# HGRN2 score levels 2, 8 and 32 as 32-column matmuls on the array's four column groups

## The chip, the cores and the metric

The kernel runs on one core of a Trainium2 chip. The metric is the device time of one execution in microseconds. Three runs of the kernel before gave 2279.91, 2280.7 and 2283.08 us; the median is 2280.7 us. One further execution was profiled. It is the source of all rows of the trace below.

## The reference, cut to what matters

One layer of a hybrid decoder is run for 256 prompt tokens and 8 x 8 sample tokens, 320 columns in all. It has two token mixers, an mLSTM with 4 heads and an HGRN2 with 8 heads, fed by one input projection and followed by branch, output and feed-forward projections. The change lies in the scores `a` of the HGRN2 heads:

```python
G = jnp.cumsum(lfc, axis=2)
rel = G[:, :, :, None, :] - G[:, :, None, :, :]
rel = jnp.where(causal[:, :, None], rel, -jnp.inf)
a = jnp.sum(qc[:, :, :, None, :] * jnp.exp(rel) * kc[:, :, None, :, :], axis=-1)
o = jnp.einsum('bhts,bhsv->bhtv', a, ic) + jnp.einsum('bhtk,bhkv->bhtv', qc * jnp.exp(G), S)
```

For a pair of tokens s < t the weight is the product of the forget gates between them, channel by channel, times q of t and k of s, summed over 128 channels.

## The kernel before, in words

All weights are streamed once. A weight tile of 128 output columns comes in two units of 128 x 1024 numbers. ScalarE rounds a unit to a high part (`wh`, line 334), VectorE forms the low part (`wl`, line 504), and TensorE multiplies both parts by the 320 token columns, three products for each of the 16 steps over 2048 rows. So a unit is 24 matmuls with a moving operand of 320 columns. This stream, called the main stream here, runs from the first microseconds to nearly the end. Everything else is slipped in between.

The order of all engines is written out by a planner when the program is built. Each piece of side work is a generator (a chain) that yields requests: an engine with a cost in ns and the instructions, a wait for an event, or a buffer of a pool. `Sched.pump` is called after each step of the main stream. A side matmul is put into TensorE's order when the planner's clock has passed the time at which its inputs are due plus a lead of 450 ns. The planner's costs only set the order; on the chip, semaphores keep it.

The HGRN2 heads run while their input projections are streamed. The eight heads follow one another about every 49 us (line 1434 runs at 467.5, 517.5, 566.1 and so on to 759.8 us). For head h the chain `h_scan` forms cumulative gate products by doubling. On the way it writes, for the blocks B = 2, 8 and 32 of `QUADS`, a buffer `y` of 1024 columns from the pool `yb`, which holds one buffer. Columns 0 to 383 of it are k times its gate products, columns 384 on are q times its gate products, six blocks of B columns for every group of four blocks. The chain `h_a` turns each `y` into scores: for each 128 tokens one full matmul (lines 1542 to 1544) with the 128 columns of k as weights and 192 columns of q as moving operand (96 columns for the 64 sample tokens, which only B = 2 has). These are fp32 matmuls, which the profile shows as two passes each. A 128 x 192 product holds many entries that belong to no group of four blocks; three masked copies per level (line 1556) move the wanted ones from the bank to `at`. A level takes one bank of the pool `sbank` of six, makes its matmuls, gives `y` back, copies, gives the bank back, and the next level follows. A fifth buffer, for B = 128, comes from the same pool.

Around it stand `h_state`, which holds one bank and takes four more at once for the sample states, and the main stream's evictions, which have two banks of their own (`mbank`). When the last mLSTM head is done, `m_after` calls `carve_h`, which lays out the HGRN2 buffers over tiles that the mLSTM part used. There the tile `rxb`, which takes the memory `rx` of mLSTM states, is laid out for the branch inputs `bah` that `ev_o` writes after the heads.

Of the kernel before, what the change touches and what calls it, by code (L numbers as in the profile page):

```python
# [246 lines left out]
def post(ev):  # L247
    return ("set", ev)
# [19 lines left out]
PE_4 = 400.0  # L268
PE_C = 2000.0
PE_H = 1250.0  # L270


def cap(ap, off, dims):
# [22 lines left out]
class Program:  # L296
# [49 lines left out]
    def carve(self):  # L346
        class Part:
            def __init__(self, ap, lo=0):
                self.ap, self.o, self.end = ap, lo, ap.shape[1]

            def __call__(self, n, parts=128):
                self.o += n
                assert self.o <= self.end, (self.o, self.end)
                return self.ap[:parts, self.o - n:self.o]

            def three(self, a, b):
                return self(a * b).rearrange("p (a b) -> p a b", a=a)

        self.Part = Part
        A, B, C, R = Part(self.f1), Part(self.f2), Part(self.f3), Part(self.ra[:, 0:6400])  # L360

        self.hs = Pool([A(2048) for _ in range(3)])

        self.qk = Pool([A.three(4, 320) for _ in range(2)])
        self.vr = Pool([A(1280)])
        B2 = Part(self.f2a)
        self.kw = Pool([B2.three(2, 320)])
        self.bc = Pool([B2(712) for _ in range(2)])
        self.eb0 = B(512)
        self.eb = Pool([self.eb0])  # L370
        self.stg = Pool([B2(256), B(256)])
        self.qn0 = B(ODD + 256)
        self.qn = Pool([self.qn0])
        X = Part(self.rx)
        self.cb = Pool([C(512) for _ in range(6)] + [X(512) for _ in range(8)])
        self.hb0 = C.three(3, 512)
        self.hb = Pool([self.hb0])
        self.qz0 = C(ODD + 512)
        self.qz = Pool([self.qz0])
        self.tst = Pool([B(512)])  # L380
        self.tail = Pool([B(64) for _ in range(2)])
        self.tst2 = B(320)
        self.ss0 = self.ra[:, 6384:6384 + ODD + 256]
        self.shl = Pool([(R(384), R(384), self.ss0)])
        self.vhl = Pool([R(2048).rearrange("p (x n) -> p x n", x=2)])
        self.vs = Pool([R(512)])
        R(1024)
        self.kst = Pool([R.three(2, 256)])
        self.vst = Pool([R.three(2, 512)])

        A, B = Part(self.f1, 6144), Part(self.f2)
        self.sb = Pool([A.three(4, 256) for _ in range(2)])
        self.at = Pool([A(512) for _ in range(2)])
        self.yb0 = A(1024)
        self.yb = Pool([self.yb0])
        self.hstg0 = [B(128) for _ in range(2)]
        self.hstg = Pool(self.hstg0)
        self.on0 = B.three(3, 256)
        self.on = Pool([self.on0])
        self.ho = Pool([B(256) for _ in range(2)])  # L400
        self.tail2 = Pool([B(64) for _ in range(2)])
        R2 = Part(self.ra, 5120)
        self.hkst = Pool([R2.three(2, 128)])
        self.phl = Pool([(R2(512), R2(512))])
        self.hvs = Pool([self.ra[:, 6400:6656]])
        self.late = [B(320) for _ in range(4)]
        self.sg0 = B(320)
        self.sg = Pool([self.sg0, self.tst2])
        B = Part(self.f2, 2000)
        self.sr = Pool([B(320) for _ in range(2)])  # L410

        B = Part(self.f2)
        self.tmp = Pool([B(320) for _ in range(3)])
        self.xr = Pool([B(320) for _ in range(4)])

    def carve_h(self):
        C = self.Part(self.pool.tile([128, F3], F32, name="f3h", tag="f3"))
        qz = C(ODD + 256)
        self.hqz = Pool([qz])
        pp = C(512)  # L420
        self.pp = Pool([pp])
        self.ktk = Pool([C(256)])
        R = self.Part(self.pool.tile([128, 2320], F32R, name="f2r", tag="f2a"))
        self.it = Pool([[R(512) for _ in range(2)] for _ in range(2)])
        as_ = R(ODD + 256)
        self.ats = Pool([as_])
        for x in (qz, as_.bitcast(F32), *(x[:, 0:64] for x in self.hstg0), pp[:, 480:512], self.yb0[:, 320:384]):
            self.nc.gpsimd.memset(x, 0.0)
        self.rh = self.pool.tile([128, 512], F32R, name="rh", tag="rh")
        self.hvst = Pool([self.rh.rearrange("p (a b) -> p a b", a=2)])  # L430
        X, R = self.Part(self.pool.tile([128, 4096], F32R, name="rxb", tag="rx")), self.Part(self.ra)
        self.bah = Slices([(X if j < 12 else R)(TOK) for j in range(KT)])
        self.bal = Slices([R(TOK) for _ in range(KT)])
        now = self.s.t["pe"]
        self.hs.free.append((now, C(2048)))
        self.sb.free += [(now, C.three(4, 256)) for _ in range(2)]
        self.sg.free += [(now, self.sg0), (now, self.late[0])]
        self.sr.free.append((now, self.late[1]))
        self.ld = Pool(self.late[2:])

    def carve_m(self):

# [171 lines left out]
    def before(self, i, t):  # L614
        s = self.s
        kind, h, c = t[:3]
        if kind == "mv" and c == 0:
            s.until(lambda: self.vr.free and self.qk.free)
            self.m_start(h)
            self.vr.free.sort(key=lambda x: x[0])  # L620
            self.mh[h]["vr"] = self.vr.free.pop(0)[1]
        elif kind == "hf":
            s.until(lambda: self.hs.free)
            if h == 0:
                s.spawn(self.m_after(), 0)
            self.h_start(h)
        elif kind == "o" and h == 0:
            s.until(lambda: all(m["end"].t is not None for m in self.mh))
        elif kind == "hg" and h == 0:
            s.until(lambda: all(m["end"].t is not None for m in self.hh))  # L630
            self.carve_m()
            self.carve_b()
            f2 = self.pool.tile([128, 2320], F32, name="f2l", tag="f2a")
            B = self.Part(f2)
            for pool in (self.sg, self.sg, self.sr, self.ld, self.ld, self.ld):
                pool.free.append((s.t["pe"], B(320)))
            B = self.Part(f2)
            self.lnb = [B(320) for _ in range(7)]
# [22 lines left out]
    def start(self):  # L661
# [40 lines left out]
        self.bc_ev = [Ev() for _ in range(MH)]  # L702
        self.mh = [dict(end=Ev()) for _ in range(MH)]
        self.hh = [dict(end=Ev()) for _ in range(HH)]
        self.m_all = Ev()
        self.ba_ev = [Ev() for _ in range(KT)]
        self.bb_ev = [Ev() for _ in range(KT)]
        self.mg_ev = [Ev() for _ in range(KT)]
# [682 lines left out]
    def h_start(self, h):  # L1391
# [2 lines left out]
        a = m["set"] = self.hs.free.pop(0)[1]  # L1394
        a = self.Part(a)
        m["qk"], m["fs"], m["iv"] = a.three(2, 384), a.three(2, 320), a(640)
        for n in ("kst", "f", "q", "lv", "o", "pre8", "suf", "I", "V", "av", "SP", "S", "aT", "qz", "ist", "sdone", "got", "ld"):
            m[n] = Ev()
        m["i"] = [Ev(), Ev()]
        m["Y"] = [Ev() for _ in range(5)]  # L1400
# [60 lines left out]
    def h_scan(self, h):  # L1461
# [23 lines left out]
        for n, B in enumerate(QUADS):  # L1485
# [14 lines left out]
            yield from join(2 * B, T)  # L1500
            if B == 2:
                yield post(m["pre8"])
        y = m["y"][4] = yield acq(self.yb)
        for i in range(2):
            yield ("dve", dve(128), lambda: v.tensor_tensor(y[:, 128 * i:128 * i + 128], qk[:, i, 128 * i:128 * i + 128], fs[:, i, 128 * i:128 * i + 128], ALU.mult))
        yield post(m["Y"][4])
# [4 lines left out]
    def h_a(self, h):  # L1511
# [22 lines left out]
        yield ("dve", dve(192, True) + 150, lambda: v.copy_predicated(a3[:, :, 1:128:2], mk, b[:, TOK:TOK + 192].rearrange("p (a t) -> p a t", a=3)))  # L1534
        yield rel(self.sbank, b)
        at_mask = 64
        for n, B in enumerate(QUADS):
            yield wait(m["Y"][n + 1])
            y = m["y"][n + 1]
            b = yield acq(self.sbank)  # L1540
            w, g = (3 if B == 2 else 2), 128 // (4 * B)
            for i in range(w):
                k = 192 if i < 2 else 96
                yield ("pe", pe_f(k), lambda: self.mm(b[:, 192 * i:192 * i + k], y[:, 128 * i:128 * i + 128], y[:, 384 + 192 * i:384 + 192 * i + k], start=True, stop=True))
            yield rel(self.yb, y)
            for d in (1, 2, 3):
                k, o = (4 - d) * B, (0, 3, 5)[d - 1] * B
                if B == 2:
# [10 lines left out]
        y = m["y"][4]  # L1559
        b = yield acq(self.sbank)  # L1560
        yield ("pe", pe_f(128), lambda: self.mm(b[:, 0:128], y[:, 0:128], y[:, 128:256], start=True, stop=True))
        yield rel(self.yb, y)
        yield ("act", act(128, True), lambda: self.A(at[:, 384:512], b[:, 0:128]))
        yield rel(self.sbank, b)
        yield post(m["aT"])

    def h_i(self, h):
        m = self.hh[h]
# [252 lines left out]
    def ev_o(self, j, c, b):  # L1821
        v = self.nc.vector
        g = yield acq(self.sg)
        r = yield acq(self.sr)
        yield from self.sigmoid(b[:, :TOK], g, r, ((self.mbank, b),))
        yield rel(self.sr, r)
        x = yield from self.fetched("o", j)
        yield ("dve", dve(TOK), lambda: v.scalar_tensor_tensor(g, g, self.vec[:, V_MLG + j:V_MLG + j + 1], x, ALU.mult, ALU.mult))
        yield rel(self.ld, x)
        if j >= 12:  # L1830

            yield wait(*(m[e] for m in self.hh for e in ("av", "sdone")))
        yield from self.split(g, self.bah[:, j, :], self.bal[:, j, :])
        yield rel(self.sg, g)
        yield post(self.ba_ev[j])
# [400 lines left out]
```

## Time and profile before

| what | value |
|---|---|
| median of three runs | 2280.7 us |
| span of the profiled execution | 2278.2 us |
| TensorE matmul busy | 2268.4 us |
| VectorE busy | 1426.4 us |
| ScalarE busy | 1014.8 us |
| stage of the HGRN2 heads | about 445 to 817 us |

The profiled execution has no time of its own beside its span, which runs from its first to its last instruction; the runs' median is 2.5 us longer. In the rows below, PE is TensorE's matmuls, PEld its weight loads, DVE VectorE, ACT ScalarE. A matmul's row gives the partitions and columns of the weights in use (`128*32`) and the shape of the moving operand. Line 340 is the helper through which nearly all matmuls pass, so groups are told apart by their operands: `xh`, `xl` with `wh`, `wl` is the main stream; `bank<-f 128*128 128x192` and `128x96` are the score matmuls of the change, as `y` lies in the tile `f`.

In a timeline a row's duration contains the latency of a pipelined matmul. What a matmul costs the stream is read from the distance between starts.

### The profile page before, as it was taken

How to read it: one execution, taken by the hardware profiler on the slowest of the kernel's cores; microseconds unless marked ns; L12 is line 12 of the kernel's file. 1: busy time of each engine (PE TensorE's matmuls, PEld its weight loads, DVE VectorE, ACT ScalarE, POOL GpSimd, SP SyncE). 2: the span in 40 equal slices, each digit the busy share in tenths (PEclk: the TensorE clock that was granted, in tenths of full speed). 3: DMA queues.
4: the chain of work that ended last, by engine and by line, in shares of the span. 5: the costliest groups of instructions: out<-in, count | busy, mean ns of one | idle time of the engine just before them, and what ended most of it. 6: DMA issues, size and time to landing. Idle time of an engine off the chain costs nothing.

```text
span 2278.2 us, 39090 instructions
## 1 busy us (share of the span) xinstructions
PE 2268.4 (100%) x15546; PEld 2231.5 (98%) x15546; DVE 1426.4 (63%) x2490; ACT 1014.8 (45%) x1574; POOL 13.5 (1%) x42
## 2 busy tenths in 40 slices
PE   9999999999999999999999999999999999999998
PEld 9999999999999999999999999999999999999998
DVE  6767566798888877555555769444444444444566
ACT  5434444455555565444433447333433343234434
POOL 0000000000000000000000000000000000000000
PEclk9999999999999999999999999999999999999999
DMA  7887887677667764444555644444444444444644
GB/s 243 304 262 258 247 273 235 215 222 227 210 208 222 220 207 171 171 172 171 181 173 196 202 154 148 150 154 150 148 148 149 154 151 148 148 149 153 197 150 158
DMA packets 251167, 432.88 MB, mean 190 GB/s; under 512 B 106844, under 2 KB 146916, under 8 KB 250984
## 3 DMA queue, kind: packets, MB, share of 16 engines
q1 hardware_dynamic: 250088, 427.24, 56.5%
q0 software_dynamic: 896, 3.15, 0.5%
q8 instruction: 122, 2.00, 0.4%
q14 instruction: 61, 0.50, 0.1%
HBM read 377.30 MB, written 53.00 MB: 189 GB/s over the span
## 4 chain that ended last, share of the span: by engine, by line
PE 96%; DMA 1%; ACT 1%; DVE 1%; issue 0%; SPq 0%; ACTq 0%; POOL 0%; DVEq 0%; POOLq 0%
PE bank L340 96%; DMA wr<-wt 1%; ACT f3m L334 0%; ACT wh L334 0%; DVE wl L504 0%; SPq L343 0%; ACT oC L334 0%; PE bank L1117 0%; PE bank L1041 0%; DMA ksD<-ra 0%; PE bank L1315 0%; ACT f2l L334 0%; DVE f L1472 0%; ACT oS L334 0%; DVE f3m L2107 0%
## 5 line engine op out<-in xcount | busy, mean ns | idle before, releaser
L340 PE MATMUL bank<-xh,wh 128*128 128x320 f32 x2408 | 759.8, 317 | 0.0
L340 PE MATMUL bank<-xh,wl 128*128 128x320 f32 x2408 | 743.1, 310 | 0.0
L340 PE MATMUL bank<-xl,wh 128*128 128x320 f32 x2408 | 740.4, 309 | 0.0
L334 ACT ACTIVATE wh<-wr 128x1024 fp32r<-128x1024 f32 (+1 forms) x432 | 453.2, 1049 | 624.3 <-PE bank L340 571.4
L504 DVE TENSOR_TENSOR wl<-wr,wh 128x1024 fp32r<-128x1024 f32 x423 | 517.0, 1222 | 324.7 <-ACT wh L334 318.1
L340 PEld LDWEIGHTS bank<-xh,wh 128*128 128x128 f32 x2408 | 453.0, 188 | 6.1 <-issue 3.9
L340 PEld LDWEIGHTS bank<-xl,wh 128*128 128x128 f32 x2408 | 452.6, 188 | 2.6
L340 PEld LDWEIGHTS bank<-xh,wl 128*128 128x128 f32 x2408 | 452.9, 188 | 0.0
L334 ACT ACTIVATE bb<-wr 128x1024 fp32r<-128x1024 f32 x181 | 191.9, 1061 | 355.9 <-PE bank L340 340.1
L504 DVE TENSOR_TENSOR bb<-wr,bb 128x1024 fp32r<-128x1024 f32 x179 | 219.2, 1225 | 162.0 <-ACT bb L334 162.0
L340 PE MATMUL bank<-xh,bb 128*128 128x320 f32 (+1 forms) x1280 | 284.1, 309 | 0.0
L340 PE MATMUL bank<-ra,bb 128*128 128x320 f32 x1264 | 283.3, 308 | 0.0
L340 PE MATMUL bank<-rxb,bb 128*128 128x320 f32 x1112 | 255.0, 309 | 0.0
L340 PE MATMUL bank<-ra,wh 128*128 128x320 f32 x892 | 248.8, 308 | 0.0
L340 PEld LDWEIGHTS bank<-xh,bb 128*128 128x128 f32 x1280 | 214.6, 188 | 0.0
L340 PEld LDWEIGHTS bank<-ra,bb 128*128 128x128 f32 x1264 | 210.6, 188 | 0.2
L340 PE MATMUL bank<-xl,bb 128*128 128x320 f32 (+1 forms) x640 | 197.5, 309 | 0.0
L340 PEld LDWEIGHTS bank<-rxb,bb 128*128 128x128 f32 x1112 | 188.3, 188 | 0.2
L340 PE MATMUL bank<-rxb,wl 128*128 128x320 f32 x596 | 183.7, 308 | 0.0
L340 PE MATMUL bank<-rxb,wh 128*128 128x320 f32 x596 | 183.7, 308 | 0.0
L340 PEld LDWEIGHTS bank<-ra,wh 128*128 128x128 f32 x892 | 161.4, 188 | 0.0
L340 PEld LDWEIGHTS bank<-xl,bb 128*128 128x128 f32 x640 | 120.2, 188 | 0.0
(333 smaller groups left out, 2140.2 us busy)
## 6 DMA issues: line engine op xcount, KB each, us to landing
wr<-wt SPq DMA_DIRECT2D x602, 512.0 KB
rx<-C SPq DMA_DIRECT2D x34, 256.0 KB
Cs<-rx SPq DMA_DIRECT2D x34, 256.0 KB
f<-C SPq DMA_DIRECT2D x30, 256.0 KB
Cs<-f SPq DMA_DIRECT2D x30, 256.0 KB
f<-xT SPq DMA_DIRECT2D x26, 160.0 KB
f<-S SPq DMA_DIRECT2D x8, 512.0 KB
f3h<-S SPq DMA_DIRECT2D x8, 512.0 KB
```

The lines of the kernel that those rows point to most:

```text
L334: return self.nc.scalar.activation(out, in_, func, **kw)
L340: self.nc.tensor.matmul(*a, **kw)
L504: self.V().tensor_tensor(lo, raw, hi.bitcast(F32), ALU.subtract)
```

## The change

The three levels' matmuls are issued together. `h_a` waits for all three `y`, takes three banks at once, and issues 26 fp32 matmuls with 32 weight columns each in one request. The matmul of group g uses the 32 columns of k from 32 g on and writes partitions 32 g to 32 g + 31 of the bank. For B = 2 and 8 each group covers 48 columns of q, the ones that belong to its own 32 tokens; for B = 32 there are four matmuls of 64, 64, 32 and 32 columns, two of them on group 0, none on group 3. The masked copies are as before. `yb` has four buffers of 1024 columns in a new tile `ry` on the memory `rx`; B = 128 keeps the old buffer as its own pool `y4`. As `ry` now stands where `rxb` stood, `rxb`, `bah` and `bal` are laid out later, by `carve_ba`, once all heads have issued their matmuls, and `ev_o` waits for that event. One memset of the old buffer's padding is gone.

```diff
+PE_Q = 1150.0
...
-        self.yb0 = A(1024)
-        self.yb = Pool([self.yb0])
+        self.y4 = Pool([A(1024)])
...
-        X, R = self.Part(self.pool.tile([128, 4096], F32R, name="rxb", tag="rx")), self.Part(self.ra)
-        self.bah = Slices([(X if j < 12 else R)(TOK) for j in range(KT)])
-        self.bal = Slices([R(TOK) for _ in range(KT)])
+        X = self.Part(self.pool.tile([128, 4096], F32, name="ry", tag="rx"))
+        self.yb = Pool([X(1024) for _ in range(4)])
...
+    def carve_ba(self):
+
+        yield wait(*[m["Q"] for m in self.hh])
+        X, R = self.Part(self.pool.tile([128, 4096], F32R, name="rxb", tag="rx")), self.Part(self.ra)
+        self.bah = Slices([(X if j < 12 else R)(TOK) for j in range(KT)])
+        self.bal = Slices([R(TOK) for _ in range(KT)])
+        yield post(self.rx_ev)
...
         at_mask = 64
+        yield wait(*m["Y"][1:4])
+        ys = m["y"][1:4]
+        bs = yield acq(self.sbank, 3)
+        yield ("pe", PE_Q, lambda: [self.quads(B, y, b) for B, y, b in zip(QUADS, ys, bs)])
+        for y in ys:
+            yield rel(self.yb, y)
+        yield post(m["Q"])
         for n, B in enumerate(QUADS):
-            yield wait(m["Y"][n + 1])
-            y = m["y"][n + 1]
-            b = yield acq(self.sbank)
+            b = bs[n]
             w, g = (3 if B == 2 else 2), 128 // (4 * B)
-            for i in range(w):
-                k = 192 if i < 2 else 96
-                yield ("pe", pe_f(k), lambda: self.mm(b[:, 192 * i:192 * i + k], y[:, 128 * i:128 * i + 128], y[:, 384 + 192 * i:384 + 192 * i + k], start=True, stop=True))
-            yield rel(self.yb, y)
...
+    def quads(self, B, y, b):
+
+        def four(g, i, k, dims):
+            p, o = slice(32 * g, 32 * g + 32), 192 * i + k
+            self.mm(cap(b[p], o, dims), y[:, 128 * i + 32 * g:128 * i + 32 * g + 32], cap(y, 384 + o, dims), start=True, stop=True, skip_group_check=True)
+
+        for i in range(3 if B == 2 else 2):
+            if B < 32:
+                for g in range(4 if i < 2 else 2):
+                    four(g, i, 48 * g, [[1, 48]])
+            else:
+                for g, k, dims in ((0, 0, [[96, 2], [1, 32]]), (1, 32, [[96, 2], [1, 32]]), (2, 64, [[1, 32]]), (0, 160, [[1, 32]])):
+                    four(g, i, k, dims)
...
     def ev_o(self, j, c, b):
...
         yield rel(self.ld, x)
+        yield wait(self.rx_ev)
         if j >= 12:
```

More of the change, by code (lines that the diff above doesn't have):

```diff
@@ L426, in carve_h @@
         self.ats = Pool([as_])
-        for x in (qz, as_.bitcast(F32), *(x[:, 0:64] for x in self.hstg0), pp[:, 480:512], self.yb0[:, 320:384]):
+        for x in (qz, as_.bitcast(F32), *(x[:, 0:64] for x in self.hstg0), pp[:, 480:512]):
             self.nc.gpsimd.memset(x, 0.0)
@@ L626, in before @@
             self.h_start(h)
+            if h == HH - 1:
+                s.spawn(self.carve_ba(), 0)
         elif kind == "o" and h == 0:
@@ L704, in start @@
         self.hh = [dict(end=Ev()) for _ in range(HH)]
-        self.m_all = Ev()
+        self.m_all, self.rx_ev = Ev(), Ev()
         self.ba_ev = [Ev() for _ in range(KT)]
@@ L1396, in h_start @@
         m["qk"], m["fs"], m["iv"] = a.three(2, 384), a.three(2, 320), a(640)
-        for n in ("kst", "f", "q", "lv", "o", "pre8", "suf", "I", "V", "av", "SP", "S", "aT", "qz", "ist", "sdone", "got", "ld"):
+        for n in ("kst", "f", "q", "lv", "o", "pre8", "suf", "I", "V", "av", "SP", "S", "aT", "qz", "ist", "sdone", "got", "ld", "Q"):
             m[n] = Ev()
@@ L1502, in h_scan @@
                 yield post(m["pre8"])
-        y = m["y"][4] = yield acq(self.yb)
+        y = m["y"][4] = yield acq(self.y4)
         for i in range(2):
@@ L1561, in h_a @@
         yield ("pe", pe_f(128), lambda: self.mm(b[:, 0:128], y[:, 0:128], y[:, 128:256], start=True, stop=True))
-        yield rel(self.yb, y)
+        yield rel(self.y4, y)
         yield ("act", act(128, True), lambda: self.A(at[:, 384:512], b[:, 0:128]))
```

## The prediction, as put on record before the result was known

> **What bounds the kernel now.** I read the page's busy times and its chain first, then the list of TensorE's waits, then the chain in order of time, then the stage of the heads by windows.
>
> ```profile
> span 2278.2 us, 39090 instructions
> PE 2268.4 (100%) x15546; PEld 2231.5 (98%) x15546; DVE 1426.4 (63%) x2490; ACT 1014.8 (45%) x1574; POOL 13.5 (1%) x42
> PE 96%; DMA 1%; ACT 1%; DVE 1%; issue 0%; SPq 0%; ACTq 0%; POOL 0%; DVEq 0%; POOLq 0%
> PE bank L340 <- POOL ones L668: 1.0, 1, 1.0
> PE bank L1041 <- ACT f L334: 0.4, 1, 0.4
> PE bank L1117 <- DVE f2a L1059: 0.3, 1, 0.3
> 840.24 1413.27 PE bank L340 x9628
> 440.00:790.00 350.00, 349.91 (x2481) 342.24 (x2480) 296.99 (x793) 183.40 (x377) 3.92 (x16) 1.00 0.70 218
> ```
>
> TensorE is busy for all of the span but 9.8 us, its waits sum to 1.7 us, and 96% of the chain that ends last is its matmuls. A busy PE need not be at its peak, so the pace is checked: 1413.27 us for 9628 matmuls is 146.8 ns from start to start, at 320 columns each. In the stage of the heads (the last row; the columns are PE, PEld, DVE, ACT, POOL, then the granted clock and the DMA share) TensorE is still full, at clock 1.00, with VectorE next at 297 of 350 us. So what leaves TensorE's stream there leaves the end time, as long as nothing else becomes late.
>
> **What is removed.** Seven fp32 matmuls per head. The profile has two passes for each, so 96 rows of 192 columns are 48 matmuls, six for each of eight heads, and 16 rows of 96 columns are one per head.
>
> ```profile
> L340 PE MATMUL bank<-f 128*128 128x192 f32 x96 | 23.5, 327 | 0.0
> L340 PE MATMUL bank<-f 128*128 128x96 f32 x16 | 2.9, 260 | 0.0
> ...
> 462.51 0.31 PE L340 MATMUL bank<-xh,wl 128*128 128x320 f32 x1
> 462.65 0.49 PE L340 MATMUL bank<-f 128*128 128x192 f32 x2
> 462.84 0.44 PE L340 MATMUL bank<-xh,wh 128*128 128x320 f32 x1
> 463.12 0.31 PE L340 MATMUL bank<-xl,wh 128*128 128x320 f32 x1
> 463.27 0.31 PE L340 MATMUL bank<-xh,wl 128*128 128x320 f32 x1
> ...
> 458.21 0.30 PE L340 MATMUL bank<-xh,wl 128*128 128x320 f32 x1
> 458.35 0.36 PE L340 MATMUL bank<-f 128*128 128x96 f32 x2
> 458.49 0.39 PE L340 MATMUL bank<-xh,wh 128*128 128x320 f32 x1
> 458.72 0.31 PE L340 MATMUL bank<-xl,wh 128*128 128x320 f32 x1
> 458.87 0.31 PE L340 MATMUL bank<-xh,wl 128*128 128x320 f32 x1
> ```
>
> The busy figures of the groups overlap with the main stream, so I take the delay instead. From 462.51 to 463.27 are 0.76 us, in which three steps of the main stream take 3 x 0.147 = 0.44: the 192-column matmul costs 0.32 us. The 96-column one costs 458.87 - 458.21 - 0.44 = 0.22. The last 192-column matmul of the stage (788.24 to 789.01 around the row at 788.39 below) costs 0.33. So per head 6 x 0.325 + 0.22 = 2.17 us, and 17.4 us for eight heads.
>
> **What is added.** One lump of 26 matmuls with 32 weight columns per head. The trace has no such lump of 48 columns, but two kinds with 256 and 320, both fp32 on the same four column groups: the sample states of the heads, and the gate rows at the start.
>
> ```profile
> 478.33 0.31 PE L340 MATMUL bank<-xh,wl 128*128 128x320 f32 x1
> 478.56 1.07 PE L340 MATMUL bank<-f,f3h 128*32 128x256 f32 x16
> 479.56 0.51 PE L340 MATMUL bank<-rh,ra 32*128 32x256 f32 x8
> 480.00 0.41 PE L340 MATMUL bank<-xh,wh 128*128 128x320 f32 x1
> 480.25 0.31 PE L340 MATMUL bank<-xl,wh 128*128 128x320 f32 x1
> ...
> 18.61 2.36 PE L340 MATMUL bank<-f 128*32 128x320 f32 x32
> 20.91 0.57 PE L340 MATMUL bank<-xh,ra 128*128 128x320 f32 x2
> ...
> 478.56 0.42 PE L340 MATMUL bank<-f,f3h 128*32 128x256 f32 x4
> L340 PE MATMUL bank<-f,f3h x16: 379/379/403, 478.6 to 479.3; 128*32 128x256 f32 x16
> ```
>
> The groups do run at once: a window of 50 ns inside the first lump finds four matmuls in flight, which together take 0.42 us where one takes 0.403, so four started within some 20 ns. A lump's length is thus that of its fullest group. Group 0 had 4 passes of 256 columns in 479.56 - 478.56 = 1.00 us, and 8 passes of 320 columns in 20.91 - 18.61 = 2.30 us. Two equations, columns times a slope plus a fixed part: (2.30 - 1.00) / (2560 - 1024) = 0.846 ns per column and pass, and 0.13 us fixed. Before the lump the stream loses 478.56 - 478.33 - 0.147 = 0.09, and after it 480.25 - 480.00 - 0.147 = 0.10 (the next weights weren't loaded ahead). Together 0.33 us per lump, whatever is in it.
>
> In the new lump group 0 is the fullest: 3 x 48 columns for B = 2, 2 x 48 for B = 8 and 2 x (64 + 32) for B = 32, 432 columns, in two passes 864, times 0.846 is 0.73 us. If a short pass has 2 or 3 ns of its own that the slope from long passes doesn't show, 18 passes add 0.05. I take 0.75 + 0.33 = 1.08 us. Lower end: 0.73 + 0.19 = 0.92, if the fixed 0.13 inside the lump, which was read from long passes, didn't come with short ones. Upper ends: the next weights take 403 - 379 = 24 ns at a lump's first pass; if a pass of 48 columns hid none of that, 17 more times 24 ns is 0.41, so 1.49. If the groups didn't overlap at all for short passes, all 1248 columns in two passes take 2496 x 0.846 = 2.11, plus 0.33 is 2.44. I take the near end, as the passes of 41 ns are still longer than the 24 ns to be hidden.
>
> **What is moved, and costs nothing.** The masked copies, the products that fill `y`, and their transfers keep their number; VectorE's and ScalarE's work isn't changed. With four `y` buffers VectorE needn't wait for a level's matmuls before it fills the next. The tile `ry` needs the old `rx` free, and the later `rxb` needs the last lump done:
>
> ```profile
> L343 SPq DMA_DIRECT2D Cs<-rx x2: 333/333/333, 413.0 to 415.0; - x2
> 450.24 0.49 DVE L1493 TENSOR_TENSOR f<-f 128x320 f32<-128x320 f32 x1
> ...
> 788.24 0.31 PE L340 MATMUL bank<-xh,wl 128*128 128x320 f32 x1
> 788.39 0.49 PE L340 MATMUL bank<-f 128*128 128x192 f32 x2
> ...
> 789.01 0.31 PE L340 MATMUL bank<-xh,wl 128*128 128x320 f32 x1
> L334 ACT ACTIVATE rxb<-f x2: 454/463/472, 794.6 to 801.0; 128x320 fp32r<-128x320 f32 x2
> L1556 DVE COPY_PREDICATED f<-lmask,bank x72: 195/323/525, 459.6 to 790.9; 128x192 f32<-128x192 uint8 x16, 128x128 f32<-128x128 uint8 x16, 128x64 f32<-128x64 uint8 x16, 128x240 f32<-128x240 uint8 x8
> L504 DVE TENSOR_TENSOR wl<-wr,wh 128x1024 fp32r<-128x1024 f32 x89 | 108.4, 1218 | 20.3 <-ACT wh L334 16.7 <-PE bank L340 1.9 <-DMA f2r<-sD 0.9
> ```
>
> The last transfer out of `rx` is issued at 415.0 us and the first `y` is written at 450.24: 35 us apart. The last of the old matmuls starts at 788.39 and `rxb` is first written at 794.6: 6 us, and the lump stands where the level of 32 stood. Were that cover gone, ScalarE would wait at the head of its queue with the next `wh` behind it, once per run, for a microsecond or two. Within the lump, TensorE can wait for VectorE's last product for B = 32; it waited at each level before and the trace has no such wait, so I charge none. Three banks at once instead of one can hold up `h_state`, whose four banks come from the same six; it then issues a little later, in a stream that is full anyway.
>
> **Sum.** Per head 2.17 - 1.08 = 1.09 us, times eight is 8.7 us. The profiled span goes from 2278.2 to 2269.5, and the runs, 2.5 us above it, from 2280.7 to 2272.0. Own range of this case: 2270.5 (a lump of 0.92 gives 2270.7) to 2273.5.
>
> **The rivals.**
>
> Weight loads that short passes don't hide. The lump is 1.49, the gain (2.17 - 1.49) x 8 = 5.4, the time 2275.3. For it: no pass under 256 columns on 32 weight columns is in the trace. Against: the loads are short.
>
> The change doesn't do what it says: passes of 48 columns follow one another instead of running on four groups. The lump is 2.44, the time 2280.7 + 8 x 0.27 = 2282.9. Against it stands the overlap shown above, in the same precision.
>
> VectorE takes the place of TensorE. After the lump nine copies stand together, 9 x 0.323 = 2.9 us, and the next low part `wl` (1.218 us) may queue behind them, with TensorE waiting for it. Against: VectorE has 350 - 297 = 53 us free in the stage, and the freed time only takes 9 of them; the same copies ran before between the same low parts. If most of the gain goes back this way, 2279.5.
>
> The slower one: the supply of instructions sets the lump's length, not the columns. The densest supply that the rows show is the sample lump, 24 passes from 478.56 to 480.00, 60 ns each. At that rate 52 passes take 3.12 us, and with 0.19 before and after 3.31; each head loses 1.14, the time is 2289.8. It decides from 2.17 / 52 = 42 ns per pass on. For it: 52 weight loads and 52 passes in 0.75 us are four times denser than anything in the trace. Against: that lump has an explanation without it (its columns), and four started within 20 ns, though these may have been queued in advance.
>
> The Trainium skill, "TensorE: Matmul & The Clock Gate", section "Wait — 56ns, not 53.3ns?", has a milder form of this, and it speaks against the change: with hardware decoding off, the sequencer spends about 62 ns per matmul, which binds once the array's work per matmul is shorter. As an estimate from that page, 26 x 62 ns plus my 0.33 make a lump of 1.94 us and a time of 2278.9. No run here shows 26 short matmuls in a row, so the trace neither bears it out nor excludes it.
>
> **How the numbers follow.** The forecast has 0.80, the unhidden loads 0.08, one after another 0.03, VectorE 0.04, the supply 0.05. The predicted time is 2272.0. The range goes from 2269.5, a microsecond below the shortest lump for the scatter of the runs, to 2277.0, which takes in the unhidden loads. A measurement of this kernel tells 0.2%, 4.6 us, from no change. Faster by more than that are the forecast and half to two thirds of the unhidden loads, which lie near the bound: 0.84. Within: the rest of these, one after another, VectorE: 0.11. Slower: 0.05.
>
> **What would show it.** Eight lumps of 52 passes of 32 weight columns between 455 and 790 us, each delaying the main stream by about 1.1 us from the start before to the second start after; four passes in flight at once; the rows of 192 and 96 columns gone; TensorE's waits still near 2 us in all; the stretch after the heads at 146.8 ns per matmul, as before, and starting some 9 us sooner. It is wrong if a lump lasts over 1.6 us, if the starts of its passes are spread at an even 25 ns or more, or if TensorE waits for `wl` between 455 and 800 us.

## The result, and the profile after

The kernel after takes 2269.69 us (median of five runs, 2268.46 to 2273.18), the kernel before 2279.91 us in five runs beside it (2279.19 to 2283.08). The ratio is 0.9953, with a 95% interval from 0.9942 to 0.9964: 10.2 us less, between 8.2 and 13.2. Two more sets of five runs of the kernel after, on two chips, gave 10.4 and 10.2 us less than the kernel before on the same chip.

The page of the kernel after, its first line and its busy times:

```profile
span 2268.1 us, 39724 instructions
PE 2259.7 (100%) x15850; PEld 2220.4 (98%) x15850; DVE 1424.2 (63%) x2490; ACT 1014.0 (45%) x1574; POOL 13.4 (1%) x41
```

TensorE is still busy for all of the span but 8.4 us, with 304 more passes than before: eight times 52 - 14. VectorE and ScalarE have as many instructions as before. The list of TensorE's waits:

```profile
PE bank L341 <- POOL ones L677: 1.0, 1, 1.0
PE bank L1126 <- DVE f2a L1068: 0.4, 1, 0.4
PE bank L341 <- DVE wl L511: 0.3, 1, 0.3
```

They still sum to 1.7 us, and none of them lies between 455 and 800 us. The long stretch after the heads in the chain of work that ended last (start, us, count):

```profile
836.44 1408.44 PE bank L341 x9595
```

Here 1408.44 us for 9595 matmuls are 146.8 ns each, the pace of before. The row starts only 3.8 us sooner than before, but it holds 33 matmuls fewer, so its start is not the same point of the work; it ends 8.6 us sooner (2244.88 after 2253.51). The lump of the second head, in TensorE's timeline, and a window of 20 ns inside it:

```profile
494.81 0.31 PE L341 MATMUL bank<-xh,wl 128*128 128x320 f32 x1
495.05 0.96 PE L341 MATMUL bank<-ry 128*32 128x48 f32 x52
495.94 0.41 PE L341 MATMUL bank<-xh,wh 128*128 128x320 f32 x1
496.19 0.31 PE L341 MATMUL bank<-xl,wh 128*128 128x320 f32 x1
...
495.11 0.38 PE L341 MATMUL bank<-ry 128*32 128x48 f32 x18
```

The delay is read as in the prediction, from the start before the lump to the second start after it, less two steps of 0.147: 496.19 - 494.81 - 0.29 = 1.09 us. The eight lumps lie between 1.080 and 1.088. Eighteen passes are in flight within 20 ns, as a pass's record contains its latency. In the single records the lump's first sixteen passes begin in bursts of four, 6 or 7 ns apart.

How much of this arrives behind the heads is read between two points of the main stream that both kernels have. Ahead of the heads I take the 2501st matmul of the main stream, behind them the first product of the branch inputs in `rxb`. The rows before and after; the `rxb` row gives its first and its last start:

```profile
436.92 0.31 PE L340 MATMUL bank<-xl,wh 128*128 128x320 f32 x1
L340 PE MATMUL bank<-rxb,wh x596: 307/308/309, 905.1 to 2241.6; 128*128 128x320 f32 x199
```

```profile
437.52 0.31 PE L341 MATMUL bank<-xl,wh 128*128 128x320 f32 x1
L341 PE MATMUL bank<-rxb,wh x596: 307/308/309, 896.5 to 2233.0; 128*128 128x320 f32 x199
```

The first product of `rxb` starts 8.6 us sooner, and so does the last, 1336.5 us later. But the stretch ahead of the heads happened to take 0.6 us longer in the trace after, so the stage itself is 9.2 us shorter. That first stretch differs from execution to execution, the stage hardly, as the traces of the repeats below show (us):

| trace | 2501st main matmul | first `rxb` product | between them | last matmul's start to the end |
|---|---|---|---|---|
| before | 436.92 | 905.10 | 468.18 | 8.39 |
| before, first repeat | 439.94 | 907.76 | 467.82 | 8.25 |
| before, second repeat | 438.14 | 905.92 | 467.78 | 8.27 |
| after | 437.52 | 896.46 | 458.94 | 6.90 |
| after, first repeat | 436.81 | 895.84 | 459.03 | 6.92 |
| after, second repeat | 437.51 | 896.45 | 458.94 | 6.90 |

The stage is 8.8 to 9.2 us shorter. In the two profiles the span is 10.1 us shorter. What is left, 1.5 us, comes after the last matmul has started, at 2269.79 us before and 2261.15 after: from there to the span's end are 8.39 us before and 6.90 after. Two windows, the 2 us ahead of that start and the 4 us behind it, before and after (the last two figures are the DMA share and GB/s):

```profile
2267.79:2269.79 2.00, 2.00 (x14) 1.84 (x12) 2.00 (x4) 2.00 (x5) 0.00 (x0) 1.00 0.43 162
2269.79:2273.79 4.00, 0.38 (x2) 0.00 (x0) 0.72 (x2) 1.61 (x4) 0.00 (x0) 1.00 1.01 382
```

```profile
2259.15:2261.15 2.00, 2.00 (x13) 1.84 (x12) 2.00 (x4) 2.00 (x5) 0.00 (x0) 1.00 0.87 336
2261.15:2265.15 4.00, 0.38 (x2) 0.00 (x0) 0.71 (x2) 1.62 (x4) 0.00 (x0) 0.92 1.00 371
```

The end is not TensorE's but the transfers': they run at the full rate for 4 us after the last matmul. In the 2 us ahead of it the kernel before used 0.43 of the DMA engines, the kernel after 0.87, so that 2 x 0.44 = 0.88 us of transfer more was still to be done. The other 0.6 us of the 1.5 weren't divided further. SP's queue shows why there was nothing to transfer. Before, with the long issue once more in a window of its own in the second row (the `x2` row ahead of it holds this issue and the next one):

```profile
2266.11 0.34 SPq L343 DMA_DIRECT2D Cp<-oC  x1
2267.20 1.97 SPq L343 DMA_DIRECT2D y<-f3m  x2
2269.26 0.41 SPq L343 DMA_DIRECT2D Sp<-oS  x1
2269.86 1.20 SPq L343 DMA_DIRECT2D y<-f3m  x2
...
2267.20 1.49 SPq L343 DMA_DIRECT2D y<-f3m  x1
```

After, the same stores:

```profile
2257.46 0.34 SPq L344 DMA_DIRECT2D Cp<-oC  x1
2258.56 1.43 SPq L344 DMA_DIRECT2D y<-f3m  x2
2260.13 0.33 SPq L344 DMA_DIRECT2D Sp<-oS  x1
2261.22 0.88 SPq L344 DMA_DIRECT2D y<-f3m  x2
...
2258.56 0.33 SPq L344 DMA_DIRECT2D y<-f3m  x1
```

Both `y` stores stand 2.59 us ahead of the last matmul's start. Before, SP took 1.49 us to issue this one; after, 0.33. The DMA queues of the kernel before in the window from 2266.5 to 2268.4 us have one packet on queue q8 (packets, MB, share of 16 engines):

```profile
q8 instruction: 1, 0.02, 5.7%
```

This packet of 16 KB of instructions took 5.7% of 16 engines' 1.9 us, that is 1.73 us. By its record it started 3.20 us before the last matmul, and the store's issue ended 0.37 us after it. In the kernel after, the last such packet started 15.56 us before the last matmul, and no store's issue was lengthened by it. Whether this explains the 1.5 us was tried below.

### The profile page after: what moved, and what is told of

It is laid out like the page before. It is cut to its first block, busy times and chain, and to the rows that moved or that the text cites. A ratio compares the mean times of both kernels' runs of the same rounds, so it can differ in the third digit from the quotient of the medians.

```text
span 2268.1 us, 39724 instructions
## 1 busy us (share of the span) xinstructions
PE 2259.7 (100%) x15850; PEld 2220.4 (98%) x15850; DVE 1424.2 (63%) x2490; ACT 1014.0 (45%) x1574; POOL 13.4 (1%) x41
## 4 chain that ended last, share of the span: by engine, by line
PE 95%; DMA 2%; DVE 1%; ACT 1%; SPq 0%; issue 0%; ACTq 0%
PE bank L341 94%; DMA wr<-wt 1%; DVE wl L511 0%; ACT f3m L335 0%; DMA f<-xT 0%; SPq L344 0%; DMA Cs<-rx 0%; ACT wh L335 0%; DMA rx<-wt 0%; ACT oC L335 0%; DVE f L1566 0%; PE bank L1126 0%; PE bank L1324 0%; DVE f L1481 0%; PE bank L1050 0%
```

## The experiments

The first four ran on one chip, where the kernel before took 2280.74 us in 33 runs, 0.5 to 1.1 us more than on the others; each is compared with that.

**The matmuls or their place.** The buffers, the waits and the three banks are those of the change, but the seven full matmuls of before stand in the lump.

```diff
-        yield ("pe", PE_Q, lambda: [self.quads(B, y, b) for B, y, b in zip(QUADS, ys, bs)])
+        yield ("pe", 2130.0, lambda: [self.whole(B, y, b) for B, y, b in zip(QUADS, ys, bs)])
...
+    def whole(self, B, y, b):
+        for i in range(3 if B == 2 else 2):
+            k = 192 if i < 2 else 96
+            self.mm(b[:, 192 * i:192 * i + k], y[:, 128 * i:128 * i + 128], y[:, 384 + 192 * i:384 + 192 * i + k], start=True, stop=True)
```

> The buffers, the waits and the one request per head are those of the change, but the request holds the seven matmuls of before, with 128 weight columns, in place of the 26. (Four small memsets on GpSimd keep the padding of the new buffers at zero.) If the gain comes from the matmuls alone, these cost about 2.17 us per head again and the time is that of the kernel before, 2279.9 within 1 us. If the moved buffers, the wait for all three levels or the new order gave a part of it (some 1.5 us of the 10.2 are not in the predicted sum), the time is about 2278.4. If they cost something, it is over 2281.

```profile
493.00 0.31 PE L341 MATMUL bank<-xh,wl 128*128 128x320 f32 x1
493.15 2.34 PE L341 MATMUL bank<-ry 128*128 128x192 f32 x14
...
495.47 0.31 PE L341 MATMUL bank<-xl,wh 128*128 128x320 f32 x1
```

2279.37 us, ratio 0.9995 (0.9986 to 1.0003). The lump delays the stream by 495.47 - 493.00 - 0.29 = 2.18 us by these rounded rows (2.170 to 2.175 over the heads). With the old matmuls the runs can't tell the change from no change, so nearly all of the gain is the matmuls', and the moved buffers and waits cost nothing that shows.

The trace shows more than the runs. The stage from the 2501st main matmul to the first `rxb` product is 467.5 us, 0.3 to 0.7 less than before: gathered, the seven old matmuls are a little cheaper than one by one. And the end after the last matmul's start is 7.35 us, not 8.25 to 8.39, though the matmuls are those of before. TensorE has 12 instructions more here (31214 in place of 31202, for more waits), and the last q8 packet starts 4.56 us before the last matmul instead of 3.20. The `y` store that was stuck is issued in the usual time, and the store ahead of it is lengthened by 0.27 us, to 0.37 us behind the packet's end:

```profile
2267.59 0.61 SPq L344 DMA_DIRECT2D Cp<-oC  x1
...
2268.68 0.33 SPq L344 DMA_DIRECT2D y<-f3m  x1
```

So about 1.0 us of the shorter end doesn't need the new matmuls.

**The fixed part.** Each level is a request of its own.

```diff
-        yield ("pe", PE_Q, lambda: [self.quads(B, y, b) for B, y, b in zip(QUADS, ys, bs)])
+        for B, y, b in zip(QUADS, ys, bs):
+            yield ("pe", 580.0, lambda: self.quads(B, y, b))
```

> The same 26 matmuls per head, but each level is a request of its own, so three lumps per head. If a lump costs a fixed 0.33 us beside its columns, the three take 0.33 + 0.24, 0.33 + 0.16 and 0.33 + 0.33 us, together 1.73 in place of 1.08, and the time is 5.2 us above the changed kernel's 2269.7, 2274.9. If the fixed part is not one per lump, the time stays at 2269.7.

The first level's 20 passes in one head:

```profile
538.75 0.30 PE L341 MATMUL bank<-xh,wl 128*128 128x320 f32 x1
538.99 0.45 PE L341 MATMUL bank<-ry 128*32 128x48 f32 x20
...
539.62 0.31 PE L341 MATMUL bank<-xl,wh 128*128 128x320 f32 x1
```

The three parts cost 0.573, 0.503 and 0.662, together 1.74 us, 0.65 more than in one lump: twice the fixed 0.33. The time is 2276.91 us, ratio 0.9984 (0.9975 to 0.9993). The expected absolute time was missed by 2 us, 0.8 of it because this chip was slower for the kernel before too. The fixed part is read from the lumps; the runs are a weak check. In the trace the stage is some 3.6 us shorter than before and the end, at 6.93 us, some 1.4 shorter, together 5.0; the runs gain 3.8, with an interval from 1.6 to 5.7.

**The supply of instructions.** The 26 matmuls are issued twice in a row.

```diff
-        yield ("pe", PE_Q, lambda: [self.quads(B, y, b) for B, y, b in zip(QUADS, ys, bs)])
+        yield ("pe", PE_Q + 750.0, lambda: [self.quads(B, y, b) for _ in range(2) for B, y, b in zip(QUADS, ys, bs)])
```

> The 26 matmuls of a head are issued twice in the same lump. The second pass writes the same numbers. If the columns of the fullest group set the body, it is 0.75 us more per lump, 1.83 us, and the time is 6.0 us above 2269.7, 2275.7. If the supply of instructions begins to bind with 52 matmuls in a row, a lump is well above 1.83 us and the time above 2277.

```profile
491.37 0.31 PE L341 MATMUL bank<-xh,wl 128*128 128x320 f32 x1
491.61 1.74 PE L341 MATMUL bank<-ry 128*32 128x48 f32 x104
...
493.53 0.31 PE L341 MATMUL bank<-xl,wh 128*128 128x320 f32 x1
```

The lump is 493.53 - 491.37 - 0.29 = 1.87 us: the second 52 passes add 0.78, which is 15 ns per pass, close to the 0.75 that the columns of group 0 make. Nothing slows down within 104 passes, so no limit on the supply of instructions shows there. 2277.28 us, ratio 0.9986 (0.9978 to 0.9995).

**The order within the lump.** The same 26 matmuls, sorted by group: first all of group 0, then all of group 1, and so on. (`parts` is the loop of `quads`, returning each matmul's group and arguments in place of issuing it.)

```diff
-        yield ("pe", PE_Q, lambda: [self.quads(B, y, b) for B, y, b in zip(QUADS, ys, bs)])
+        yield ("pe", 2440.0, lambda: [self.mm(*x, start=True, stop=True, skip_group_check=True) for _, *x in sorted(
+            [x for B, y, b in zip(QUADS, ys, bs) for x in self.parts(B, y, b)], key=lambda x: x[0])])
```

> The same 26 matmuls in one lump, ordered by column group: all nine of group 0, then all of group 1, 2 and 3. If matmuls start in program order, a group's second must wait for its first and holds up the other groups behind it, so the groups follow one another: 1248 columns in two passes at 0.846 ns and 0.33, 2.44 us per lump, and a time of 2269.7 + 8 x 1.36 = 2280.5. If each group has a queue of its own, the lump stays at 1.08 us and the time at 2269.7.

```profile
491.92 0.31 PE L341 MATMUL bank<-xh,wl 128*128 128x320 f32 x1
492.16 1.98 PE L341 MATMUL bank<-ry 128*32 128x48 f32 x52
...
494.32 0.31 PE L341 MATMUL bank<-xl,wh 128*128 128x320 f32 x1
```

The lump is 2.11 us, twice that of the mixed order. That fits the first theory and not the second: groups don't run ahead from queues of their own, and a pass whose group is busy holds back those behind it. The lump is 0.33 us below the full serial length of 2.44, on average 0.11 for each of the three changes of group; what overlaps there wasn't tried. 2279.11 us, ratio 0.9993 (0.9985 to 1.0002): the gain of the stage is gone, 468.0 us as before. The 1.6 us between the medians are about what the end gives, 6.93 us here as well.

**Which group sets the length.** Every head gets another part of the lump; head 0 is left as it is. (`x[2][0]` is a matmul's group, `x[0]` its B, `x[1]` its place in the level.)

```diff
+        todo = [(B, n, x) for B, y, b in zip(QUADS, ys, bs) for n, x in enumerate(self.parts(B, y, b))]
+        if h == 1:
+            todo = [x for x in todo if x[0] != 32 or x[1] % 4 != 3]
+        elif h == 2:
+            todo = [x for x in todo if x[0] != 32 or x[1] % 4 != 2]
+        elif h == 3:
+            todo = [x for x in todo if x[0] != 32]
+        elif h == 4:
+            todo = [x for x in todo if x[2][0] == 0]
+        elif h == 5:
+            todo = [x for x in todo if x[2][0] < 2]
+        elif h == 6:
+            todo = [x for x in todo if x[0] == 8]
+        elif h == 7:
+            todo.sort(key=lambda x: -x[0])
```

> The lump differs from head to head; in six heads matmuls are left out, so part of the scores is missing. Each lump is read from the profile, as delay of the main stream from the start before to the second start after. Two theories. A: 0.33 us and the columns of the fullest group, two passes, 0.846 ns each (2 to 3 ns more per pass). B: 0.33 us and 29 ns for each matmul, whatever its group. Head 0, all 26: A 1.08, B 1.08. Head 1, without group 0's second matmuls at B = 32, 24 in all: A 0.97, B 1.03. Head 2, without group 2's at B = 32, 24: A 1.08, B 1.03. Head 3, without B = 32, 18: A 0.75, B 0.85. Head 4, group 0 alone, 9: A 1.05 to 1.08, B 0.59. Head 5, groups 0 and 1 alone, 16: A 1.08, B 0.79. Head 6, B = 8 alone, 8: A 0.50, B 0.56. Head 7, all 26 with B = 32 first: both 1.08.

Head 4, group 0 alone, and head 6, only B = 8:

```profile
635.56 0.31 PE L341 MATMUL bank<-xh,wl 128*128 128x320 f32 x1
635.80 0.96 PE L341 MATMUL bank<-ry 128*32 128x48 f32 x18
...
636.93 0.30 PE L341 MATMUL bank<-xl,wh 128*128 128x320 f32 x1
...
726.51 0.30 PE L341 MATMUL bank<-xh,wl 128*128 128x320 f32 x1
726.74 0.38 PE L341 MATMUL bank<-ry 128*32 128x48 f32 x16
...
727.30 0.31 PE L341 MATMUL bank<-xl,wh 128*128 128x320 f32 x1
```

The eight lumps cost 1.09, 0.97, 1.08, 0.74, 1.08, 1.09, 0.50 and 1.09 us. The 18 passes of group 0 alone (head 4) take as long as all 52. Leaving out a matmul of group 2 (head 2) changes nothing, leaving out group 0's last ones (head 1) takes 0.12 off. The length is 0.33 and the fullest group's columns, in every head; a cost per matmul (theory B) misses three of the eight by 0.1 to 0.5 us.

**The kernel after, again.** It repeats the gain in another set of runs, with a profile of its own.

> The changed kernel once more, on another chip or at another time. The lumps of the two traces account for 8 x (2.19 - 1.08) = 8.9 us and the medians differ by 10.2. If the rest is the scatter between executions (above all in the stores after the last matmul, 8.4 us in the one trace before and 6.9 in the one after), this run gives a difference between 8 and 10 us. If it belongs to the change, it is again 10 us or more, and the stretch after the last matmul is again near 6.9 us.

2269.34 us, ratio 0.9954 (0.9940 to 0.9967). The lumps are 1.080 to 1.088, and from the last matmul's start to the end are 6.92 us.

**An evener lump.** Group 0's second matmul for B = 32 goes to group 3, which had none; its copy then reads partitions 96 to 127.

```diff
+                if B == 32 and d == 3:
+                    yield ("dve", dve(64, True), lambda: v.tensor_copy(cap(at[0:32], 96, [[128, 2], [1, 32]]), cap(b[96:128], 160, [[192, 2], [1, 32]])))
+                    continue
...
-                for g, k, dims in ((0, 0, [[96, 2], [1, 32]]), (1, 32, [[96, 2], [1, 32]]), (2, 64, [[1, 32]]), (0, 160, [[1, 32]])):
+                for g, k, dims in ((0, 0, [[96, 2], [1, 32]]), (1, 32, [[96, 2], [1, 32]]), (2, 64, [[1, 32]])):
                     four(g, i, k, dims)
+                o = 192 * i + 160
+                self.mm(b[96:128, o:o + 32], y[:, 128 * i:128 * i + 32], y[:, 384 + o:384 + o + 32], start=True, stop=True, skip_group_check=True)
```

> The changed kernel with group 0's second matmul at B = 32 (32 columns, for each 128 tokens) put on group 3, which has nothing at that level. Its result lands on partitions 96 to 127, so the last masked copy of that level becomes a plain copy of 32 partitions from there. If the fullest group sets the lump, group 0 falls from 432 to 368 columns, as many as group 1 has, and the lump from 1.08 to 0.97 us: 0.9 us off the time, which the traces can show and the medians hardly. If all 26 matmuls count alike, the lump stays at 1.08.

```profile
494.62 0.31 PE L341 MATMUL bank<-xh,wl 128*128 128x320 f32 x1
494.86 0.84 PE L341 MATMUL bank<-ry 128*32 128x48 f32 x52
...
495.88 0.31 PE L341 MATMUL bank<-xl,wh 128*128 128x320 f32 x1
```

The lump is 0.97 us (0.966 to 0.974): the 64 columns fewer on group 0, in two passes at 0.846 ns, are 0.11. Eight heads give 0.9 us (the stage of the trace is 0.5 to 0.6 shorter), which the runs can't tell: 2270.06 us, ratio 0.9957 (0.9943 to 0.9970), beside the kernel after on the same chip:

> The changed kernel beside the even one on the same chip: lumps of 1.08 us, some 0.9 us above it, and 9 to 10 us below the kernel before.

2269.84 us, ratio 0.9958 (0.9945 to 0.9970), and 6.90 us from the last matmul's start to the end.

**Is the late end part of the kernel before, or scatter?** The kernel before was profiled twice more.

> The kernel before, for its stretch after the last matmul. If that stretch differs from execution to execution, it lies anywhere from 6.9 to 8.4 us. If the change shortens it, it is again near 8.4 us.

> A second such look, with the same expectation: 6.9 to 8.4 us where the stretch varies by itself, 8.4 us where it belongs to the kernel.

In the first of them, the store's issue in SP's timeline, and q8 among the DMA queues between 2269.0 and 2271.5 us:

```profile
2269.86 1.37 SPq L343 DMA_DIRECT2D y<-f3m  x1
```

```profile
q8 instruction: 1, 0.02, 3.7%
```

The packet took 1.48 us (3.7% of 16 engines' 2.5 us). From the last matmul's start to the end are 8.25 and 8.27 us, and both times the same store takes 1.37 and 1.39 us and ends 0.38 and 0.33 us after the packet. So it belongs to the kernel, not to one execution. The single times, 2282.52 and 2280.69 us, say no more.

**Whose instructions are in that packet.** First theory: SP's own. Ten more loads of 128 bytes are put on SP's queue at the start of the kernel before, so that SP's packets would shift.

```diff
+        for i in range(10):
+            yield ("sp", 620, lambda: self.dma(self.spare[0:MH, 8 * i:8 * i + 8], d["m0"]))
```

> The kernel before, with ten more tiny loads (4 x 8 numbers, into a tile that nothing reads) in SP's queue near the start. TensorE's matmuls are those of before. In all three traces of the kernel before, a store of the output is stuck in SP's queue for 1.4 to 1.5 us, 2.6 us before the last matmul, until 0.4 us after a 16 KB transfer of the instruction queue; in the changed kernel that transfer comes 12 us sooner. If it is SP's own instructions that are fetched there, ten more of them move the transfer to an earlier point: the stretch after the last matmul falls from 8.2 to 8.4 us to some 6.9 to 7.4, and the time by 1.0 to 1.4 us against the kernel before. If the fetch is another engine's, or the stretch belongs to the order of the kernel before, it stays at 8.2 to 8.4 us and the time where it was.

The theory fell: the packet stays at 3.18 us before the last matmul, the store still takes 1.34 us, and the end is 8.14 us behind. 2280.16 us, ratio 1.0002 (0.9993 to 1.0011).

Second theory: TensorE's. The kernel before has 122 packets of 16 KB on q8 and 31202 TensorE instructions (15546 weight loads, as many passes, 110 waits and the like), some 256 for a packet; the kernel after has 124 and 31819. Forty more matmuls of 48 columns, 160 instructions, are put at the start of the kernel before.

```diff
+        for i in range(40):
+            x = 32 * (i % 4)
+            self.mm(self.gbank[x:x + 32, 0:48], self.ones[:, 0:32], self.ones[:, 0:48], start=True, stop=True, skip_group_check=True)
```

> The kernel before, with forty more matmuls (32 weight columns, 48 columns, on the four column groups) at the very start, before the first data are there; nothing reads their result. Ten more loads in SP's queue had left the 16 KB transfer of the instruction queue where it was, 3.2 us before the last matmul. Its period of 18.8 us is that of 128 main matmuls. If it is TensorE's instructions that are fetched, forty more matmuls move it: the store 2.6 us before the last matmul is issued in 0.33 us again, and the stretch after the last matmul is some 6.9 to 7.4 us in place of 8.1 to 8.4. The time falls by less than that, since the forty take up to a microsecond or two themselves. If the fetch is neither engine's doing, the stretch stays at 8.1 to 8.4.

```profile
2267.90 1.42 SPq L343 DMA_DIRECT2D y<-f3m  x2
2269.47 0.33 SPq L343 DMA_DIRECT2D Sp<-oS  x1
...
2267.90 0.33 SPq L343 DMA_DIRECT2D y<-f3m  x1
```

The last q8 packet now starts 20.1 us before the last matmul, the store is issued in 0.33 us, and the end comes 7.09 us behind instead of 8.3. With more to compute than before, the kernel takes 2278.80 us beside 2280.23, ratio 0.9993 (0.9984 to 1.0002): the medians differ by 1.4 us, near the 1.0 to 1.3 that the stretch lost against the four traces with the packet at its old place (8.14 to 8.39), though the runs alone couldn't tell it from nothing. Over all traces: where the last packet starts 3.1 to 3.2 us before the last matmul (four traces), the end takes 8.14 to 8.39 us; where it starts earlier (ten traces), 6.90 to 7.35.

## Why the prediction was right or wrong

**What bounds the kernel: right.** TensorE's stream set the end of the heads' stage, and what left it arrived: the stage is 8.8 to 9.2 us shorter, of 8.7 forecast. (That the two profiles differ by 8.6 at the first product of `rxb` is luck: 0.6 us of scatter ahead of the heads lies in it.)

**What is removed and added: right, one term a little small.** 2.17 us a head were to go, read from two matmuls of 192 columns and one of 96. Over the whole trace before, 46 of the 48 with 192 columns can be read, and cost 0.33 us on average (0.318 to 0.392), the eight with 96 columns 0.22: 2.21 a head. Gathered in a lump the same matmuls cost 2.17. Eight times 2.21 less 1.08 is 9.0 us, which is what the stage lost. The lump was to cost 1.08 and costs 1.080 to 1.088. Its two parts hold as well: 0.33 us fixed, by splitting it in three, and the fullest group's columns at 0.846 ns in two passes, by the heads with parts of it and by the evener lump. The 0.05 us for short passes was needed too: doubling the lump added 0.78, not 0.73.

**What is moved, and costs nothing: right for the stage, wrong for the end.** With the old matmuls the moved buffers and waits cost nothing that shows, TensorE waits for nothing between 455 and 800 us, and the last lump starts at 774.1 us, 11 us before `rxb` is first written:

```profile
L335 ACT ACTIVATE rxb<-f x3: 454/454/472, 785.7 to 799.4; 128x320 fp32r<-128x320 f32 x3
```

The step that failed is the **sum**. "The profiled span goes from 2278.2 to 2269.5" subtracts the lumps' gain and takes all that follows the heads as it was. That end stood in it at no change, without a reason. But near the end, some 1480 us behind the last lump, a stall of the kernel before went away: the change puts 617 instructions more into TensorE's stream, two packets and 105 instructions, so the packets fall elsewhere. In the main stream 256 instructions are 128 matmuls with their weight loads, 18.8 us at 146.8 ns each; single distances between packets lie between 14 and 23 us. As an estimate from these numbers: before, the packet ahead of the last started 25.95 us ahead of the last matmul, so the last was due 7.2 us ahead of it; it came 4 us later, in the midst of the last stores, and why it was late is open. 105 instructions more put the due point 7.7 us earlier, at 14.9; the packet is found at 15.56. The end after the last matmul's start shrinks from 8.39 to 6.90 us. The forty matmuls at the start, which move the packet and leave the heads as they were, take 1.0 to 1.3 us of that; the last 0.2 us between their 7.09 and 6.90 weren't traced.

The account: forecast were 2272.0, measured 2269.69, so 2.3 us less. 0.8 us are the base: the three runs shown had the median 2280.7, the five beside the kernel after 2279.91. (The 2.5 us that the prediction put between a span and the runs compared different executions; in single executions with both on record they are 1.7 to 2.1.) The other 1.5 us are the gain, 10.2 instead of 8.7. The traces give 0.3 us more in the stage and 1.2 to 1.5 us in the end, 10.2 to 10.5 in all, so the end is most of it. The runs' interval, 8.2 to 13.2 us, can't check this to the tenth. The result lies just inside the range of 2269.5 to 2277.0 given for all cases, and below the 2270.5 of the likeliest case's own range, whose lower bound had a shorter lump as its only reason.

**The rivals.** *Unhidden weight loads* asked for a lump of 1.49: it is 1.08. *One after another* is not so in the mixed order, but it happens when the order allows it: sorted by group, the same matmuls take 2.11. The code's inner loop over the groups is what avoids it, which the prediction didn't see. *VectorE*: no wait for `wl` in the stage. *The supply of instructions* would decide from 42 ns per pass on: two lumps in a row ran at 15 ns. This decides about the rule of the Trainium skill ("TensorE: Matmul & The Clock Gate", section "Wait — 56ns, not 53.3ns?") as well: 26 more matmuls took 0.78 us, 30 ns each and not 62, so its case isn't met here. The same section has starts never closer than about 25 ns; with four column groups, one pass per 15 ns was measured.

## What to carry to other kernels

A lump of small matmuls on column groups costs a fixed part (0.33 us here) and its fullest group, if the program's order goes around the groups; so gather them, mix the groups, and even out the fullest. Where the end of a kernel is a run of stores, look at it by itself: an edit far away can shift TensorE's instruction packets into or out of it, and a microsecond gained or lost there says nothing of the edit. Before the whole gain is ascribed to the change, compare the changed stage from a point just ahead of it to one just behind it: the time since the start of the span isn't enough, as the same kernel reached the point ahead of the heads at 436.9 us in one execution and at 439.9 in another.

## What the runs showed of the hardware

A transfer of one engine's instructions can go with a late DMA issue on another engine. In the profile of the kernel before, 89 of SP's 1305 issues start while a q8 packet is on its way; 26 of them take over 0.45 us and end 0.32 to 0.43 us after the packet does, as the `y` store at the end. Of SP's 77 issues over 0.6 us, 23 are of this kind, though a packet is on its way for only 6% of the span. Of the others in that position, 60 take less than 0.45 us, most of them the usual 0.33; what tells the two apart, and what the issue waits for, wasn't found. All of TensorE's waits sum to 1.7 us, so the other lengthened issues cost the kernel next to nothing; at the end of the kernel one cost 1.0 to 1.3 us.

The Trainium skill ("Runtime: NRT & Kernel Launch", section "Instruction fetch mechanics") says that an engine's instructions are fetched in blocks of 16 KiB, 256 instructions, over a queue of the engine's own, and that the cost is mostly hidden. The trace agrees on the block (122 packets of 16 KB for 31202 instructions), and TensorE's list of waits has none for them. A cost to another engine isn't in that section; the runs show one.
